# A LayerNorm over channels in a two-layer encoder: from transposes to sums by products with a constant matrix, with part of a weight's preparation moved to GpSimd

## The chip, the cores and the metric

One core of one Trainium2 chip runs the whole program. It has five engines with a queue each, and each queue is worked off in order: TensorE (PE in the profile; PEld is its loading of the stationary operand), VectorE (DVE), ScalarE (ACT), GpSimd (POOL) and SyncE (SP), which here issues the DMAs. They wait for each other by semaphores. The metric is the device time of one execution in microseconds (us); lower is better.

## The reference

Two layers over 256 tokens with 1024 features, in float32. Each layer is a SwiGLU feed-forward block (half step), a gated pair of token mixers side by side, a second SwiGLU block and a gated input embedding. The part that matters here is the convolution branch of the mixers, which ends in a LayerNorm over its 512 channels:

```python
def layer_norm(x, g, b, eps=1e-5):
    mu = jnp.mean(xf, axis=-1, keepdims=True)
    var = jnp.mean(jnp.square(xf - mu), axis=-1, keepdims=True)
    y = (xf - mu) * lax.rsqrt(var + eps)
    return (y * g + b)
...
        y_attn = window_attention(q, k, v, sink[i], rel_bias) @ w_attn_out[i]
        c_val, c_gate = jnp.split(c, 2, axis=-1)
        c = c_val * jax.nn.sigmoid(c_gate)
        c = depthwise_conv(c, conv_w[i], conv_b[i])          # 31 taps
        c = jax.nn.silu(layer_norm(c, conv_ln_g[i], conv_ln_b[i]))
        y_conv = c @ w_conv_out[i]
        g_attn, g_conv = jnp.split(jax.nn.sigmoid(g), 2, axis=-1)
        h = h + (g_attn * y_attn + g_conv * y_conv) @ w_o[i]
```

## The kernel before

**Layout.** Activations stand with features on the 128 partitions and the 256 tokens along the free axis, so a block of 128 features is a 128x256 tile. The 512 channels of the convolution are four such blocks, y[:, 0..3, :].

**Precision.** Matmuls run on float32r operands, and each float32 operand is split in a high part (a rounding copy on ACT) and a low part (the rest, by a subtraction on DVE); a product is three matmuls: high by high, high by low, low by high. The helper split does this for activations (line 489 is the subtraction: y_l, sum_l, ym_l). For weights the class Weights does it. A weight arrives by DMA in a buffer raw (five of them), ACT writes w_hi (line 136), DVE w_lo (line 137). A piece marked shared has its w_lo made by POOL instead, in four quarters (line 125). `ws.get()` hands out a piece and prepares pieces up to LOOK = 6 ahead, less `ws.rest`; `ws.behind` names an instruction behind which these preparations are put in their engines' queues.

**What sets the order.** The queues are filled by a scheduler that works from priorities and estimated times; where the code calls `keep_in_program_order` or `issue_after`, it is bound. Matmuls of one product (`group`) are followed by an evacuation that is put off until the first part of the next product.

**The mixers (function mix), in the order of TensorE.** Inner products for the convolution (ps_c), keys, values and queries, then the 16 gate blocks in pairs (ps_g; DVE multiplies them into g at line 910, ACT takes the sigmoid later in `squash`), between which the attention is worked off (ps_s, ps_pt, ps_o; o_h and o_l are the split of its result). Meanwhile DVE runs the 31 convolution taps for four blocks (line 669), 124 operations, the last tap of each block writing y. After the last gates come:

- attn_out(0, 2, 4, 6): the attention's output product in four groups of 24 matmuls (ps_ao), each followed by DVE's step g <- ps_ao * g (line 987).
- conv_out(0, 2, 4, 6): the convolution's output product in four groups of 24 (ps_co), reading y_h and y_l, each followed by two DVE steps (g <- ps_co * g, line 1061; the sum with the attention's share, line 1062) and the split into ym_h (ACT) and ym_l (DVE).
- mix_out: the product with w_o (ps_wo, 192 matmuls), reading ym; its first two blocks run over the first six of eight feature blocks each before the last two.

The LayerNorm lies between the attn_out groups. `ln_by_token`, after group 0, transposes y on TensorE so that tokens stand on the partitions (ps_yt, 8 transposes of 128x128), takes mean and variance with two statistics operations on DVE (BN_STATS, BN_AGGR), a square root on ACT over 128x2 values, a reciprocal over 128x2, and writes the normalised yn. `ln_by_channel`, half way through group 4, transposes back (ps_yc, 8 transposes), and ACT applies gain, bias and SiLU on the way out of PSUM (y, line 1028). y is split into y_h and y_l. ACT loads its function table twice for this, for Sqrt and for SiLU.

The kernel has the same scheme for RMS norms elsewhere, which the change borrows: ones_r is a 128x128 matrix of 1/1024, and two matmuls (sum_h and sum_l, ps_stat, line 455) put the sum over partitions of a 128x256 tile on every partition; a square root over 128x256 (sd, line 402) and a reciprocal over 128x256 (r_x, line 404) follow.

Of the kernel before, what the change touches and what calls it, by code (L numbers as in the profile page):

```python
# [48 lines left out]
G0, G1, G2, G3 = 56, 16, 8, 8  # L49
# [135 lines left out]
def encoder_kernel(ctx: ExitStack, tc: tile.TileContext, a: dict, out: bass.AP):  # L185
# [70 lines left out]
    def mix_specs(l):  # L256
# [28 lines left out]
        for j in range(2):  # L285
            u = ws.unit(KC, 512, w[j])
            for c in range(2):
                ws.spec(KC, 256, [(u, 0, c * 256, 0, 256)])
# [193 lines left out]
    def bcast(r, n):  # L482
        return r.unsqueeze(1).broadcast_to([P, n, T])
# [159 lines left out]
    def mix(l, u, st, xn, stat):  # L643
        cw, kg, bias, sink = (late[n] for n in ("cw", "kg", "bias", "sink"))
        with tc.tile_pool(name="mix_pool", bufs=1) as mp:
# [8 lines left out]
            last_tap = [None]  # L654

            def tap(i, t):
# [11 lines left out]
                else:  # L668
                    last_tap[0] = nc.vector.scalar_tensor_tensor(  # L669
# [139 lines left out]

            o = mp.tile([P, GROUP, P], F32, name="o")  # L810
# [58 lines left out]
            def gather(qb):  # L869
# [121 lines left out]
            yn = mp.tile([P, 2, CD], F32, name="yn", tag="sqq")  # L991

            def ln_by_token():
                mv = tmp.tile([P, 2, 2], F32, name="mv")
                ps = []
                for t in range(2):
                    ps.append(mm_tile("ps_yt"))
                    for i in range(KC):
                        turned = nc.tensor.transpose(ps[t][:, i * P : (i + 1) * P], y[:, i, t * P : (t + 1) * P], ident)
                        tc.keep_in_program_order(turned)  # L1000
                    six = tmp.tile([P, 6], F32, name="six")
                    nc.vector.bn_stats(out=six, in_=ps[t])
                    nc.vector.bn_aggr(out=mv[:, t, :], in_=six)
                rs = tmp.tile([P, 2], F32, name="rs")
                nc.scalar.activation(out=rs, in_=mv[:, :, 1], func=AF.Sqrt, bias=eps5)
                nc.vector.reciprocal(out=rs, in_=rs)
                table(AF.Silu)
                for t in range(2):
                    normed = nc.vector.tensor_scalar(
                        out=yn[:, t, :], in0=ps[t], scalar1=mv[:, t, 0:1], scalar2=rs[:, t : t + 1],  # L1010
                        op0=ALU.subtract, op1=ALU.mult,
                    )
                return (normed.ins,)
# [3 lines left out]
            def ln_by_channel():  # L1017
# [244 lines left out]
```

## Time and profile before

| | |
|---|---|
| device time, median of 3 runs | 1070.61 us (1070.31 to 1070.61) |
| the profiled execution | 1070.46 us, of which the span from the first to the last instruction is 1068.7 us |
| granted TensorE clock | 0.999 |
| busy share of the span | PE 99%, PEld 98%, DVE 76%, ACT 59%, POOL 12% |
| read from HBM | 200.46 MB, 189 GB/s over the span |

In the rows below, times are from the span's start. A timeline row gives start, length, engine, line and operation, what it writes and reads with shapes, how many instructions are merged, and in brackets the idle time before it with what ended that. A group's row gives the count, total busy time and mean duration in ns. Two instructions that follow each other directly on DVE or ACT overlap by 0.08 to 0.1 us in their records, so that the next starts before the last one's end is recorded. Chain rows stand at the ends of matmuls, timeline rows at their starts.

### The profile page before, as it was taken

How to read it: one execution, taken by the hardware profiler on the slowest of the kernel's cores; microseconds unless marked ns; L12 is line 12 of the kernel's file. 1: busy time of each engine (PE TensorE's matmuls, PEld its weight loads, DVE VectorE, ACT ScalarE, POOL GpSimd, SP SyncE). 2: the span in 40 equal slices, each digit the busy share in tenths (PEclk: the TensorE clock that was granted, in tenths of full speed). 3: DMA queues.
4: the chain of work that ended last, by engine and by line, in shares of the span. 5: the costliest groups of instructions: out<-in, count | busy, mean ns of one | idle time of the engine just before them, and what ended most of it. 6: DMA issues, size and time to landing. Idle time of an engine off the chain costs nothing.

```text
span 1068.7 us, 22087 instructions
## 1 busy us (share of the span) xinstructions
PE 1062.5 (99%) x9174; PEld 1048.2 (98%) x9174; DVE 813.2 (76%) x1234; ACT 627.3 (59%) x1043; POOL 130.4 (12%) x205
## 2 busy tenths in 40 slices
PE   9999999999999999999999999999999999999998
PEld 9999999999999999999999999999999999999998
DVE  7966666899899767666887766669998987666665
ACT  7655444777867554444774554548778675554453
POOL 0000011146301000011100000110571100000110
PEclk9999999999999999999999999999999999999999
DMA  9775555544256455555546454565433655454531
GB/s 368 269 266 178 183 205 214 190 167 158 98 205 238 182 202 184 182 201 219 188 169 223 171 198 142 214 237 197 159 130 112 227 214 216 180 192 144 218 119 40
DMA packets 30916, 202.93 MB, mean 190 GB/s; under 512 B 3552, under 2 KB 4832, under 8 KB 10464
## 3 DMA queue, kind: packets, MB, share of 16 engines
q1 hardware_dynamic: 30816, 201.52, 51.5%
q8 instruction: 72, 1.18, 0.4%
q14 instruction: 28, 0.23, 0.1%
HBM read 200.46 MB, written 1.05 MB: 189 GB/s over the span
## 4 chain that ended last, share of the span: by engine, by line
PE 92%; DVE 7%; ACT 1%; issue 0%; POOL 0%; DVEq 0%; ACTq 0%; POOLq 0%
PE ps_gu L330 43%; PE ps_fo L330 22%; PE ps_wo L330 4%; PE ps_pe L330 4%; PE ps_c L330 4%; DVE ps_y L669 4%; PE ps_g L330 2%; PE ps_ao L974 2%; PE ps_co L974 2%; PE ps_gu L343 2%; DVE s L835 1%; PE ps_pp L330 1%; DVE w_lo L137 1%; PE ps_q L779 1%; PE ps_q L778 1%; PE ps_q L777 1%
## 5 line engine op out<-in xcount | busy, mean ns | idle before, releaser
L136 ACT CAST w_hi<-raw 128x1024 fp32r<-128x1024 f32 (+2 forms) x364 | 372.7, 1031 | 354.5 <-PE ps_gu L330 198.4
L137 DVE TENSOR_TENSOR w_lo<-raw,w_hi 128x1024 fp32r<-128x1024 f32 (+2 forms) x364 | 433.9, 1199 | 187.3 <-ACT w_hi L136 187.2
L330 PE MATMUL ps_fo<-h_hi,w_lo 128*128 128x256 f32 x704 | 193.3, 275 | 0.0
L330 PE MATMUL ps_fo<-h_lo,w_hi 128*128 128x256 f32 x704 | 193.2, 275 | 0.0
L330 PE MATMUL ps_fo<-h_hi,w_hi 128*128 128x256 f32 x704 | 193.2, 275 | 0.0
L437 POOL TENSOR_TENSOR sq_acc<-sq_acc,sq 128x256 f32<-128x256 f32 x49 | 48.1, 981 | 803.3 <-ACT sq L436 803.3
L330 PEld LDWEIGHTS ps_fo<-h_lo,w_hi 128*128 128x128 f32 x704 | 131.9, 188 | 0.0
L330 PEld LDWEIGHTS ps_fo<-h_hi,w_hi 128*128 128x128 f32 x704 | 131.9, 188 | 0.0
L330 PEld LDWEIGHTS ps_fo<-h_hi,w_lo 128*128 128x128 f32 x704 | 131.9, 188 | 0.0
L330 PE MATMUL ps_gu<-xf0l,w_hi 128*128 128x256 f32 x352 | 96.9, 275 | 0.0
L330 PE MATMUL ps_gu<-xf1h,w_lo 128*128 128x256 f32 x352 | 96.9, 275 | 0.0
L330 PE MATMUL ps_gu<-xf0h,w_lo 128*128 128x256 f32 x352 | 96.9, 275 | 0.0
L330 PE MATMUL ps_gu<-xf1l,w_hi 128*128 128x256 f32 x352 | 96.9, 275 | 0.0
L330 PE MATMUL ps_gu<-xn0h,w_lo 128*128 128x256 f32 x352 | 96.8, 276 | 0.0
L330 PE MATMUL ps_gu<-xf0h,w_hi 128*128 128x256 f32 x352 | 96.8, 275 | 0.0
L330 PE MATMUL ps_gu<-xn0l,w_hi 128*128 128x256 f32 x352 | 96.8, 275 | 0.0
L330 PE MATMUL ps_gu<-xf1h,w_hi 128*128 128x256 f32 x352 | 96.8, 275 | 0.0
L330 PE MATMUL ps_gu<-xn0h,w_hi 128*128 128x256 f32 x352 | 96.7, 276 | 0.0
L669 DVE SCALAR_TENSOR_TENSOR ps_y<-cpad,cw,ps_y 128x256 f32<-128x256 f32 x232 | 95.5, 479 | 0.0
L330 PE MATMUL ps_gu<-x0h,w_hi 128*128 128x256 f32 x304 | 83.7, 275 | 0.0
L330 PE MATMUL ps_gu<-x0h,w_lo 128*128 128x256 f32 x304 | 83.7, 275 | 0.0
L330 PE MATMUL ps_gu<-x0l,w_hi 128*128 128x256 f32 x304 | 83.7, 275 | 0.0
(239 smaller groups left out, 2785.0 us busy)
## 6 DMA issues: line engine op xcount, KB each, us to landing
raw<-in_w_ffn_in_dram SPq DMA_DIRECT2D x86, 1024.0 KB, 4.9
raw<-in_w_ffn_out_dram SPq DMA_DIRECT2D x32, 896.0 KB, 4.6
raw<-in_w_in_dram SPq DMA_DIRECT2D x26, 1024.0 KB, 4.8
raw<-in_w_ffn_out_dram SPq DMA_DIRECT2D x16, 1024.0 KB, 5.3
raw<-in_w_o_dram SPq DMA_DIRECT2D x8, 1024.0 KB, 4.7
raw<-in_w_pe_gate_dram SPq DMA_DIRECT2D x8, 1024.0 KB, 4.9
raw<-in_w_q_dram SPq DMA_DIRECT2D x4, 1024.0 KB, 5.5
raw<-in_w_attn_out_dram SPq DMA_DIRECT2D x4, 1024.0 KB, 4.8
```

The lines of the kernel that those rows point to most:

```text
L136: lambda hs=hs, src=src: nc.scalar.copy(out=hs, in_=src),
L137: lambda hs=hs, ls=ls, src=src: nc.vector.tensor_tensor(out=ls, in0=src, in1=hs.bitcast(F32), op=ALU.subtract),
L330: mm = nc.tensor.matmul(ps, wa[:, k0 + k, cols], xa[:, kx, :], start=a, stop=b)
L343: mm = nc.tensor.matmul(ps, wa[:, k, :], xa[:, k, :], start=first and n == 0, stop=last and n == len(steps) - 1)
L437: nc.gpsimd.tensor_tensor(out=self.acc, in0=self.acc, in1=sq, op=ALU.add)
L669: last_tap[0] = nc.vector.scalar_tensor_tensor(out=ps if t < TAPS - 1 else y[:, i, :], in0=src, scalar=w, in1=ps, op0=ALU.mult, op1=ALU.add)
L777: nc.tensor.matmul(o_, u[0][:, kx, ts], wh[:, k, :], start=kx == 0, stop=False)
L778: nc.tensor.matmul(o_, u[0][:, kx, ts], wl[:, k, :], start=False, stop=False)
L779: nc.tensor.matmul(o_, u[1][:, kx, ts], wh[:, k, :], start=False, stop=kx == KD - 1)
L835: nc.vector.tensor_tensor_reduce(out=s[:, c, :], in0=ps[:, c, :], in1=bias[:, v * GROUP + c, off : off + T], scale=1.0, scalar=sink[:, hd ...
L974: mm = nc.tensor.matmul(ps[:, c, :], wa[:, k, c * P : (c + 1) * P], xa[:, k, :], start=(i, k) == (0, 0), stop=(i, k) == (2, KC - 1),)
```

## The change

The LayerNorm stays with channels on the partitions. Four blocks of y are added into one 128x256 tile (`over_blocks`: two, then one; DVE), the tile is split (`halve`: sum_h on ACT, sum_l on DVE) and two matmuls with ones_r give the sum over all channels on every partition (`spread`: ps_ln). `centre` subtracts the mean from y (yn, DVE, two operations on 128x512), squares on ACT, adds and halves again. `normalise` spreads the squares' sum, takes the root over 128x256 (sd, ACT), the reciprocal over 128x256 (r_ln, DVE), multiplies yn by it (DVE, two operations), applies gain, bias and SiLU from SBUF (ACT), and splits. The first sum is spread before attn_out(0), the second between attn_out(2) and attn_out(4). Table loads stay two a layer.

Besides, the first 256 columns' piece of the convolution's output weight (the first of four pieces of w_conv_out) gets its w_lo from POOL, and the points behind which weight pieces are prepared move: behind the first addition instead of the last tap, behind the centred sum's split, behind the new y's split. A gap in SBUF grows by the room of three small tiles that are gone.

```diff
-G0, G1, G2, G3 = 56, 16, 8, 8
+G0, G1, G2, G3 = 56, 64, 8, 8
...
         for j in range(2):
             u = ws.unit(KC, 512, w[j])
             for c in range(2):
-                ws.spec(KC, 256, [(u, 0, c * 256, 0, 256)])
+                ws.spec(KC, 256, [(u, 0, c * 256, 0, 256)], shared=j + c == 0)
...
+            def over_blocks(two, a, b):
+                nc.vector.tensor_tensor(out=two, in0=a, in1=b, op=ALU.add)
+                one = tmp.tile([P, T], F32, name="one", tag="sg")
+                made = nc.vector.tensor_tensor(out=one, in0=two[:, 0, :], in1=two[:, 1, :], op=ALU.add)
+                return one, made.ins
+
+            def halve(one):
+                parts = [tmp.tile([P, T], F32R, name="sum_" + part, tag="sq") for part in "hl"]
+                made = split(parts, one)
+                tc.keep_in_program_order(made[0])
+                return parts, tuple(ins.ins for ins in made)
+
+            def spread(parts):
+                ps = mm_tile("ps_ln")[:, :T]
+                for i, part in enumerate(parts):
+                    tc.keep_in_program_order(nc.tensor.matmul(ps, ones_r, part, start=i == 0, stop=i == 1))
+                return ps
...
                 made = nc.scalar.copy(out=oh[:, :, P:], in_=ov)
                 tc.keep_in_program_order(made)
+                sc["y"], _ = halve(sc.pop("y"))
                 for k in (0, 4, 8):
                     squash(k)
...
                 if i == 2 * KD - 2:
-                    ws.behind = (last_tap[0].ins,)
+                    two = tmp.tile([P, 2, T], F32, name="two", tag="gu")
+                    sc["y"], added = over_blocks(two, y[:, 0:2, :], y[:, 2:4, :])
+                    ws.behind = (added,)
                     last_gates(i)
...
-            def ln_by_token():
...
-            def ln_by_channel():
...
+            yn = mp.tile([P, KC, T], F32, name="yn", tag="sqq")
+
+            def centre():
+                ps, squares = spread(sc.pop("y")), []
+                flush()
+                for i in range(0, KC, 2):
+                    some = yn[:, i : i + 2, :]
+                    nc.vector.scalar_tensor_tensor(
+                        out=some, in0=bcast(ps, 2), scalar=-D / CD, in1=y[:, i : i + 2, :], op0=ALU.mult, op1=ALU.add
+                    )
+                    squares.append(tmp.tile([P, 2, T], F32, name="sq2", tag="gu"))
+                    tc.keep_in_program_order(nc.scalar.activation(out=squares[-1], in_=some, func=AF.Square))
+                squash(12)
+                sc["y"], made = halve(over_blocks(squares[0], *squares)[0])
+                table(AF.Sqrt)
+                return made
...
+            def normalise():
+                sd = tmp.tile([P, T], F32, name="sd", bufs=1)
+                root = nc.scalar.activation(
+                    out=sd, in_=spread(sc.pop("y")), func=AF.Sqrt, scale=D / CD, bias=eps5
+                )
+                tc.keep_in_program_order(root)
                 table(AF.Silu)
+                r = tmp.tile([P, T], F32, name="r_ln", tag="sg")
+                nc.vector.reciprocal(out=r, in_=sd)
                 for i in range(0, KC, 2):
+                    some = yn[:, i : i + 2, :]
+                    nc.vector.tensor_tensor(out=some, in0=some, in1=bcast(r, 2), op=ALU.mult)
+                    for k in range(i, i + 2):
                         act = nc.scalar.activation(
+                            out=y[:, k, :], in_=yn[:, k, :], func=AF.Silu,
+                            scale=pcol("conv_ln_g", l, k), bias=pcol("conv_ln_b", l, k),
                         )
...
-            ws.rest = 2
+            ws.rest, ws.behind = 2, centre()
             attn_out(0)
-            ws.rest, ws.behind = 2, (squash(12),) + ln_by_token()
+            ws.rest = 3
             attn_out(2)
-            ws.rest, made = 3, []
-            attn_out(4, lambda: made.extend(ln_by_channel()))
-            ws.rest, ws.behind = 2, tuple(made)
+            ws.behind = normalise()
+            attn_out(4)
             attn_out(6)
-            ws.rest = 3
```

How the queues stand around it in layer 1 (layer 2 reads alike). TensorE's queue from the last gate product on, before:

```order
L330 MATMUL ps_g<-xm0l,w_hi 128x256
L330 MATMUL ps_g<-xm0h,w_lo 128x256
L974 MATMUL ps_ao<-o_h,w_hi 128x256 x8
L974 MATMUL ps_ao<-o_h,w_lo 128x256 x8
L974 MATMUL ps_ao<-o_l,w_hi 128x256 x8
L999 MATMUL ps_yt<-ident,y 128x128 x8
```

And in the changed kernel:

```order
L330 MATMUL ps_g<-xm0l,w_hi 128x256
L330 MATMUL ps_g<-xm0h,w_lo 128x256
L826 MATMUL ps_ln<-sum_h,ones_r 128x256
L826 MATMUL ps_ln<-sum_l,ones_r 128x256
L996 MATMUL ps_ao<-o_h,w_hi 128x256 x8
L996 MATMUL ps_ao<-o_h,w_lo 128x256 x8
L996 MATMUL ps_ao<-o_l,w_hi 128x256 x8
```

The LayerNorm's first part now stands ahead of the attention output and not behind its first group; the other pair of ps_ln stands behind the second group.

VectorE's queue from the last two taps on, before:

```order
L669 SCALAR_TENSOR_TENSOR y<-cpad,cw,ps_y 128x256
L137 TENSOR_TENSOR w_lo<-raw,w_hi 128x1024
L669 SCALAR_TENSOR_TENSOR y<-cpad,cw,ps_y 128x256
L894 TENSOR_TENSOR o_l<-o,o_h 128x4x128
L894 TENSOR_TENSOR o_l<-ps_o,o_h 128x4x128
L910 TENSOR_TENSOR g<-ps_g,r_x 128x512
L987 TENSOR_TENSOR g<-ps_ao,g 128x512
L1002 BN_STATS six<-ps_yt 128x6 x2
L1003 BN_AGGR mv<-six 128x2 x2
L1006 RECIPROCAL rs<-rs 128x2
L1009 TENSOR_SCALAR yn<-ps_yt,mv,rs 128x512 x2
L137 TENSOR_TENSOR w_lo<-raw,w_hi 128x1024
```

In the changed kernel, first to the second sum:

```order
L668 SCALAR_TENSOR_TENSOR y<-cpad,cw,ps_y 128x256 x2
L811 TENSOR_TENSOR two<-y 128x512
L914 TENSOR_TENSOR o_l<-o,o_h 128x4x128
L813 TENSOR_TENSOR one<-two 128x256
L914 TENSOR_TENSOR o_l<-ps_o,o_h 128x4x128
L489 TENSOR_TENSOR sum_l<-one,sum_h 128x256
L930 TENSOR_TENSOR g<-ps_g,r_x 128x512
L1020 SCALAR_TENSOR_TENSOR yn<-ps_ln,y 128x512 x2
L1009 TENSOR_TENSOR g<-ps_ao,g 128x512
L811 TENSOR_TENSOR sq_3746<-sq_3746,sq_3749 128x512
L813 TENSOR_TENSOR one<-sq_3746 128x256
L489 TENSOR_TENSOR sum_l<-one,sum_h 128x256
```

and from there to the convolution output:

```order
L1009 TENSOR_TENSOR g<-ps_ao,g 128x512
L1040 RECIPROCAL r_ln<-sd 128x256
L1009 TENSOR_TENSOR g<-ps_ao,g 128x512
L1043 TENSOR_TENSOR yn<-yn,r_ln 128x512 x2
L1009 TENSOR_TENSOR g<-ps_ao,g 128x512
L489 TENSOR_TENSOR y_l<-y,y_h 128x512 x2
L137 TENSOR_TENSOR w_lo<-raw,w_hi 128x1024 x2
```

The preparation of the first convolution piece has left the queue, that of the second has moved behind y_l, and the step on the third ps_ao group stands between the reciprocal and the products that use it.

VectorE's queue at the end of the convolution output, with numbers: ps_co_3920, 3955 and 3988 are the second to fourth groups, ym_l0 and ym_l1 the low parts that ps_wo reads (two rows each, one for two feature blocks). Before:

```order
L1061 TENSOR_TENSOR g_3002<-ps_co_3920,g_3002 128x512
L489 TENSOR_TENSOR ym_l0_3891<-g_3002,ym_h0_3890 128x512
L1062 TENSOR_TENSOR g_3002<-g_3002 128x512
L1061 TENSOR_TENSOR g_3002<-ps_co_3955,g_3002 128x512
L1062 TENSOR_TENSOR g_3002<-g_3002 128x512
L489 TENSOR_TENSOR ym_l0_3891<-g_3002,ym_h0_3890 128x512
L1061 TENSOR_TENSOR g_3002<-ps_co_3988,g_3002 128x512
L489 TENSOR_TENSOR ym_l1_3893<-g_3002,ym_h1_3892 128x512
L1062 TENSOR_TENSOR g_3002<-g_3002 128x512
L489 TENSOR_TENSOR ym_l1_3893<-g_3002,ym_h1_3892 128x512
```

In the changed kernel, where the groups are 3925, 3960 and 3993:

```order
L1076 TENSOR_TENSOR g_3002<-ps_co_3925,g_3002 128x512
L1076 TENSOR_TENSOR g_3002<-ps_co_3960,g_3002 128x512
L489 TENSOR_TENSOR ym_l0_3892<-g_3002,ym_h0_3891 128x512
L1077 TENSOR_TENSOR g_3002<-g_3002 128x512 x2
L1076 TENSOR_TENSOR g_3002<-ps_co_3993,g_3002 128x512
L489 TENSOR_TENSOR ym_l0_3892<-g_3002,ym_h0_3891 128x512
L1077 TENSOR_TENSOR g_3002<-g_3002 128x512
L489 TENSOR_TENSOR ym_l1_3894<-g_3002,ym_h1_3893 128x512 x2
```

Before, the step on the last group had one ym_l directly behind it, the third; now it has the second, an addition, and then the third and the fourth.

More of the change, by code (lines that the diff above doesn't have):

```diff
@@ L653, in mix @@
             ws.lag = WEIGHTS_LAG
-            last_tap = [None]
             def tap(i, t):
@@ L668, in tap @@
                 else:
-                    last_tap[0] = nc.vector.scalar_tensor_tensor(
+                    nc.vector.scalar_tensor_tensor(
                         out=ps if t < TAPS - 1 else y[:, i, :], in0=src, scalar=w, in1=ps, op0=ALU.mult, op1=ALU.add
@@ L989, in attn_out @@
                 group([products], evac)
-            yn = mp.tile([P, 2, CD], F32, name="yn", tag="sqq")
-            def ln_by_token():
[L994 to L1006, printed above, removed]
-                table(AF.Silu)
[L1008 to L1013, printed above, removed]
@@ L1015, in mix @@
-            ys = tuple(rows(mp, KC, "y_" + part) for part in "hl")
-            def ln_by_channel():
-                banks = [mm_tile("ps_yc").rearrange("p (f t) -> p f t", f=2) for _ in range(2)]
-                for t in range(2):
-                    for k in range(KC):
-                        turned = nc.tensor.transpose(
-                            banks[k // 2][:, k % 2, t * P : (t + 1) * P], yn[:, t, k * P : (k + 1) * P], ident
-                        )
-                        tc.keep_in_program_order(turned)
+            yn = mp.tile([P, KC, T], F32, name="yn", tag="sqq")
@@ new lines, in centre @@
+            def centre():
[3 more added lines that the diff above has]
+                    some = yn[:, i : i + 2, :]
+                    nc.vector.scalar_tensor_tensor(
+                        out=some, in0=bcast(ps, 2), scalar=-D / CD, in1=y[:, i : i + 2, :], op0=ALU.mult, op1=ALU.add
[6 more added lines that the diff above has]
+                return made
@@ new lines, in mix @@
+            ys = tuple(rows(mp, KC, "y_" + part) for part in "hl")
+            def normalise():
[4 more added lines that the diff above has]
+                tc.keep_in_program_order(root)
+                table(AF.Silu)
+                r = tmp.tile([P, T], F32, name="r_ln", tag="sg")
+                nc.vector.reciprocal(out=r, in_=sd)
@@ L1025, in ln_by_channel @@
                 for i in range(0, KC, 2):
-                    ps = banks[i // 2]
-                    for f in range(2):
+                    some = yn[:, i : i + 2, :]
+                    nc.vector.tensor_tensor(out=some, in0=some, in1=bcast(r, 2), op=ALU.mult)
+                    for k in range(i, i + 2):
                         act = nc.scalar.activation(
-                            out=y[:, i + f, :], in_=ps[:, f, :], func=AF.Silu,
-                            scale=pcol("conv_ln_g", l, i + f), bias=pcol("conv_ln_b", l, i + f),
+                            out=y[:, k, :], in_=yn[:, k, :], func=AF.Silu,
+                            scale=pcol("conv_ln_g", l, k), bias=pcol("conv_ln_b", l, k),
```

## Prediction

> **What bounds the kernel now.** I read the page first (busy times, chain by engine), then the waits of TensorE, then the chain in order of time through the stretch that is changed, then the timelines of VectorE (DVE), ScalarE (ACT) and GpSimd (POOL) there.
>
> ```profile
> PE 1062.5 (99%) x9174; PEld 1048.2 (98%) x9174; DVE 813.2 (76%) x1234; ACT 627.3 (59%) x1043; POOL 130.4 (12%) x205
> ...
> PE 92%; DVE 7%; ACT 1%; issue 0%; POOL 0%; DVEq 0%; ACTq 0%; POOLq 0%
> ...
> PE ps_warm L218 <- POOL ones_d L211: 1.2, 1, 1.2
> PE ps_g L330 <- DVE o L884: 0.4, 2, 0.2
> ```
>
> TensorE is busy 99% of the span and is made to wait, as far as the records tell, three times for 1.6 us. So a matmul taken out shortens the kernel by its spacing, but any time for which TensorE comes to wait is added whole: there is no slack behind it. The profiled execution took 1070.46 us (span 1068.7 and 1.76 around it), 0.15 below the median of 1070.61; the sum starts from 1070.46. A change within 0.2% (2.1 us) can hardly be told from none.
>
> ```profile
> 282.96 2.73 PE ps_ao L974 x24
> 285.69 0.87 PE ps_yt L999 x8
> 286.56 4.10 PE ps_ao L974 x36
> 290.66 0.87 PE ps_yc L1021 x8
> ...
> 295.63 10.88 PE ps_co L974 x96
> 306.51 21.97 PE ps_wo L330 x192
> ...
> 336.64 0.24 PE ps_stat L455 x2
> ...
> 814.13 0.87 PE ps_yt L999 x8
> ...
> 819.11 0.87 PE ps_yc L1021 x8
> ```
>
> This chain (start, length, what) is TensorE without a break from the attention output (ps_ao) through the convolution output (ps_co) and the mixing output (ps_wo) to the next layer step. Layer 2 repeats it 528.4 us later, so everything below counts twice. A plain 128x128x256 matmul takes 10.88/96 = 0.113 us.
>
> **TensorE's own work.** Out go 16 transposes a layer: 0.87 + 0.87 = 1.74 us. In come four matmuls with the constant, like the pair ps_stat: 2 x 0.24 = 0.48. Net -1.26 a layer, -2.5 in all. This is the whole gain on offer; VectorE's convolution piece going to GpSimd frees no time on the chain by itself.
>
> **When the new sums are ready.** In the new order TensorE wants the first pair right behind the last ps_g, where ps_ao started before (282.80 on the timelines, whose starts lie 0.16 ahead of the chain's), and the second pair between the second and third ps_ao group.
>
> ```profile
> 279.29 0.47 DVE L669 SCALAR_TENSOR_TENSOR y<-cpad,cw,ps_y 128x256 f32<-128x256 f32 x1
> 279.68 1.21 DVE L137 TENSOR_TENSOR w_lo<-raw,w_hi 128x1024 fp32r<-128x1024 f32 x1
> 280.81 0.47 DVE L669 SCALAR_TENSOR_TENSOR y<-cpad,cw,ps_y 128x256 f32<-128x256 f32 x1
> 281.20 0.68 DVE L894 TENSOR_TENSOR o_l<-o,o_h 128x512 fp32r<-128x512 f32 x1
> ...
> L489 DVE TENSOR_TENSOR sum_l<-sq_acc,sum_h 128x256 fp32r<-128x256 f32 x8 | 3.4, 421 | 0.8 <-ACT sum_h L488 0.8
> L488 ACT CAST sum_h<-sq_acc 128x256 fp32r<-128x256 f32 x8 | 3.2, 406 | 6.4 <-POOL sq_acc L437 5.1 <-DVE sq_acc L553 1.2
> ...
> 272.62 5.65 POOL L125 TENSOR_TENSOR w_lo<-raw,w_hi 128x256 fp32r<-128x256 f32 x8 [1.62 <-ACT w_hi L122]
> 230.08 9.55 POOL L125 TENSOR_TENSOR w_lo<-raw,w_hi 128x256 fp32r<-128x256 f32 x12 [4.43 <-ACT w_hi L122]
> 230.35 0.75 DVE L684 TENSOR_TENSOR cpad<-sg,gu 128x256 f32<-128x256 f32 x1 [0.65 <-ACT sg L683]
> L684 DVE TENSOR_TENSOR cpad<-sg,gu x8: 410/418/755, 201.9 to 758.8; 128x256 f32<-128x256 f32 x8
> ```
>
> First pair. The w_lo that stood between the last two taps is gone (-1.13), so the second tap starts at 279.68 and ends at 280.15. Behind it stand, each 512-wide step 0.60 and each 256-wide 0.34 after the one before (durations 0.68 and 0.42): two at 280.18, o_l at 280.78, one at 281.38 (to 281.80), o_l at 281.72; ACT's sum_h 281.83 to 282.24; sum_l 282.33 to 282.75. TensorE wants sum_l at 282.80 + 0.11 = 282.91. That would just do, by 0.16. But the moved convolution piece gives POOL four more quarter operations of 5.65/8 = 0.71 behind those that end at 278.27, to about 281.1, beside two, o_l and one, which read both inputs from SBUF. No row shows these three beside POOL. The nearest is cpad: 0.42 alone, 0.75 beside POOL's w_lo. Below lies 0 (nothing collides), above 0.93 (two waits out the third quarter, 0.22, and o_l the whole fourth, 0.71). I take 0.5, a collision of cpad's size (0.34) and half of another; less the 0.16 it makes TensorE wait 0.3 (ends 0 and 0.8).
>
> [...]
>
> Second pair. TensorE comes to it at 282.80 + 0.24 + 0.4 + 5.44 = 288.88 (48 ps_ao at 0.113; 0.4 is the wait with its restart, below). The data need on ACT, behind sum_h at 282.74, three sigmoids, two squares, a sigmoid and the cast:
>
> ```profile
> 281.24 3.91 ACT L946 ACTIVATE g<-g 128x1024 f32<-128x1024 f32 x4
> 288.25 1.28 ACT L417 ACT_TABLE_LOAD   x1
> 291.35 1.02 ACT L1028 ACTIVATE y<-ps_yc,x 128x256 f32<-128x256 f32 x2 [1.82 <-PE ps_yc L1021]
> 292.40 0.62 ACT L488 CAST y_h<-y 128x512 fp32r<-128x512 f32 x1
> ...
> 293.98 0.62 ACT L488 CAST y_h<-y 128x512 fp32r<-128x512 f32 x1
> ...
> L548 ACT ACTIVATE sq<-x 128x512 f32<-128x512 f32 x2 | 1.1, 620 | 0.0
> L402 ACT ACTIVATE sd<-ps_stat,eps 128x256 f32<-128x256 f32 x8 | 3.8, 475 | 1.0 <-PE ps_stat L455 0.9
> L404 DVE RECIPROCAL r_x<-sd 128x256 f32<-128x256 f32 x8 | 14.0, 1752 | 2.5 <-ACT sd L402 2.5
> ```
>
> Sigmoids to about 285.5, squares to 286.6, then DVE's two adds (0.68, 0.42) behind its ps_ao step to 288.1, sum_h to 288.5, sum_l to 289.0: against 288.99 no wait worth counting.
>
> **The wait at the convolution output.** Behind the second pair TensorE has two ps_ao groups (5.44) and reaches ps_co at 288.88 + 0.24 + 5.44 = 294.56; its first matmul wants the first half of y_h, its third (294.8) the second. The way there: sum_h 288.5, table load 1.28 to 289.7, sd 0.48 to 290.2, the reciprocal, now of 128x256 and not of 128x2, 1.75 to 291.95. Next in DVE's queue stands the step on the third ps_ao (0.60; TensorE ends it at 291.84 and DVE can take it 0.2 later, so 0.1 is lost), and only behind it the two products with r_ln: the first ends at 291.95 + 0.1 + 0.60 + 0.68 = 293.3. Then ACT as in the rows above: from the first y to the end of the first y_h 1.67, to the end of the second 3.25 (294.60 - 291.35): 295.0 and 296.6. TensorE waits 0.4 and then until 296.6 instead of 294.8 + 0.4: 1.4 more, 1.8 in all. The old order had 1.0 to spare here (294.60 against 295.63). y is now read from SBUF and not from PSUM, which may save some hundredths on each of four; I take 1.7 (ends 1.3, if that and the queue are kind, and 2.0).
>
> **The wait at the mixing output.** The squeezed-out w_lo make DVE late through ps_co, and the new order puts DVE's four last steps differently: the second ym_l now stands behind the step on the last ps_co, and a g add before the third ym_l.
>
> ```profile
> 306.55 0.69 DVE L1061 TENSOR_TENSOR g<-ps_co,g 128x512 f32<-128x512 f32 x1 [0.37 <-PE ps_co L974]
> 307.15 0.68 DVE L489 TENSOR_TENSOR ym_l<-g,ym_h 128x512 fp32r<-128x512 f32 x1
> ...
> 306.35 0.28 PE L330 MATMUL ps_wo<-ym_h,w_hi 128*128 128x256 f32 x1
> ...
> 307.70 0.28 PE L330 MATMUL ps_wo<-ym_h,w_hi 128*128 128x256 f32 x1
> 307.89 0.38 PE L330 MATMUL ps_wo<-ym_l,w_hi 128*128 128x256 f32 x1
> 308.11 0.28 PE L330 MATMUL ps_wo<-ym_h,w_lo 128*128 128x256 f32 x1
> ```
>
> Before, ps_wo began at W = 306.35, DVE's step on the last ps_co at W + 0.20, and the ym_l that the 14th matmul reads came at W + 1.48: 307.89 - 307.70 is 0.08 more than the spacing, a wait that the list above does not even show, and the next gap is 0.22, 0.11 lost in restarting. Now W + 0.20 is followed by ym_l (0.80 to 1.48), the add (1.41) and the ym_l for the 14th matmul (2.01 to 2.70). The 8th matmul, due at W + 0.79, waits for the first of these until 1.51 (0.7); the 14th, then due at 2.3, until 2.73 (0.45). Together 1.15, less the 0.08 of before: +1.07 (ends 0.8 and 1.3).
>
> Restarts: 0.11 at each of five pauses (one at ps_ln, two at ps_co, two at ps_wo), one of them old: +0.4.
>
> **What I cost at nothing.**
>
> ```profile
> L136 ACT CAST w_hi<-raw 128x1024 fp32r<-128x1024 f32 (+2 forms) x364 | 372.7, 1031 | 354.5 <-PE ps_gu L330 198.4
> 289.92 1.21 DVE L137 TENSOR_TENSOR w_lo<-raw,w_hi 128x1024 fp32r<-128x1024 f32 x1
> raw<-in_w_o_dram SPq DMA_DIRECT2D x8, 1024.0 KB, 4.7
> ```
>
> VectorE's queue grows by the reciprocal's 1.75 and several steps of 0.4 to 0.7, less the old statistics and one w_lo; what covers it is that weight pieces are prepared ahead. The cover is thin at one place: the w_lo of the second ps_co piece comes at 296.5 + 1.03 + 1.21 = 298.7, and TensorE wants it at 296.6 + 22 x 0.113 = 299.1; any lateness would be paid whole. Later pieces come every 1.13 us, and TensorE uses one in 2.7. That w_lo was done at 291.1 before, so the load on SP's queue that reuses its buffer goes out 7.6 us later and lands at about 303.4 (4.7 each); it brings the last two of eight w_o pieces, wanted 16 us after ps_wo begins, so the loads behind it on that queue are no nearer to their use either. POOL's piece is ready 13 us before its use. The longer gap memset ahead of ones_d, for which TensorE waits at the start, costs some hundredths once; where tiles come to lie in SBUF I price at zero, as no row shows a price for it.
>
> **Sum.** A layer: -1.26 + 0.3 + 1.7 + 1.07 + 0.4 = +2.2; two layers +4.4; 1070.46 + 4.4 = 1074.9 us.
>
> **Rivals.**
> The gain comes through. All waits are covered and only -2.5 stays: 1068.0. For it speaks that the old chain had 1.0 us to spare at ps_co; against it that y_h would have to come 1.8 earlier, which is just the reciprocal's length, and the ym_l order would have to be harmless as well. It decides from the point where both waits together fall below 1.26 a layer. 7%.
> One wait alone. The convolution output waits but the mixing output doesn't (DVE could have run its adds sooner), or the other way round: -1.26 + 0.3 + 1.7 + 0.2 = +0.9, or -1.26 + 0.3 + 1.07 + 0.2 = +0.3 a layer: 1071.1 to 1072.3, no difference to speak of. Against it: the two have separate causes, both in fixed queues. 13%.
> GpSimd holds VectorE. If each of two, o_l and one waits out a quarter, the first pair waits 0.8, and a late w_lo at the second ps_co adds 0.3: +3.0 a layer, 1076.5. The rows of cpad speak for the kind, not for the number of collisions. [...] 15%.
> The likeliest, both waits and a small collision: 65%, with bounds from the low ends (-1.26 + 0 + 1.3 + 0.8 + 0.3 = +1.1, 1072.7) to the high ends without the third rival (+2.9, 1076.3).
>
> **The numbers.** 1074.9. The range of 8 in 10 takes in the likeliest case (65%), the third rival (to 1077.2) and the upper edge of the second (1071.9): 1071.9 to 1077.2. Faster by over 0.2%: 0.07; within 0.2%: 0.14; slower: 0.79.
>
> **What would show it.** In the changed kernel's list of TensorE waits: ps_co for ACT's y_h, about 1.5 to 1.8 us twice; ps_wo for DVE's ym_l, about 0.7 and 0.4 twice; ps_ln for DVE's sum_l, up to 0.8. From ps_wo to the next ps_stat nothing changes. If ps_co starts at 294.6 and runs 10.9 us without a break, the step on the reciprocal is wrong; if ps_wo still takes 22.0 us, the step on the ym_l order is.

## The result, and the profile after

The changed kernel takes 1078.16 us (median of four executions, 1076.63 to 1080.1) against 1070.56 before (1070.31 to 1070.61): a ratio of 1.0073 [1.0061, 1.0085], slower by 7.6 us. The forecast was 1074.9 (1071.9 to 1077.2): the sign is right, the time lies above the range. The profiled execution is the fastest of the four: 1076.63 us, a span of 1074.8 against 1068.7.

The page's busy times and the chain by engine:

```profile
PE 1063.2 (99%) x9150; PEld 1046.6 (97%) x9150; DVE 819.7 (76%) x1240; ACT 630.9 (59%) x1051; POOL 136.3 (13%) x213
...
PE 87%; DVE 10%; ACT 2%; DMA 0%; issue 0%; SPq 0%; DVEq 0%; ACTq 0%
```

TensorE still looks busy 99% of the time (a matmul's record is mostly 0.28 long and its spacing 0.113, so short pauses hide in that number). But the chain is TensorE for 87% instead of 92% of the span: it now runs through other engines. The list of TensorE's waits names them (total us, times, longest):

```profile
PE ps_co L996 <- ACT y_h L488: 3.2, 4, 1.1
PE ps_wo L330 <- DVE ym_l L489: 1.6, 4, 0.6
PE ps_warm L218 <- POOL ones_d L211: 1.2, 1, 1.2
PE ps_gu L343 <- ACT w_hi L136: 0.4, 1, 0.4
```

The two new waits are those that the prediction names, in both layers; the last row is a wait of 0.4 at the kernel's start. (A fifth row, 0.4 at ps_g, stands as before.) Through the changed stretch the chain, which was TensorE without a break, now reads (start, length, what):

```profile
280.94 1.22 DVE o_l L914
282.16 0.34 DVE one L813
...
283.09 0.34 DVE sum_l L489
283.44 0.04 issue
...
289.49 0.39 PE ps_ln L826
...
292.66 0.69 DVE g L1009
293.36 0.61 DVE yn L1043
...
293.99 1.10 ACT y L1045 x2
...
296.76 0.63 ACT y_h L488
...
297.43 10.97 PE ps_co L996 x94
...
310.97 20.61 PE ps_wo L330 x179
331.58 8.16 PE ps_gu L330 x72
339.74 0.24 PE ps_stat L455 x2
...
871.16 0.24 PE ps_stat L455 x2
```

The stretch begins with the last gate product. Before, TensorE's timeline has there:

```profile
282.69 0.28 PE L330 MATMUL ps_g<-xm0h,w_lo 128*128 128x256 f32 x1
282.80 0.95 PE L974 MATMUL ps_ao<-o_h,w_hi 128*128 128x256 f32 x7
```

From the last ps_g (282.81, below) to ps_stat it is 56.93 us; before, from the last ps_g (282.69) to ps_stat (336.64), 53.95. So a layer costs 2.98 more. The second layer agrees: ps_stat comes 531.42 after that of the first layer instead of 528.45, 2.97 more. With the 0.12 by which the last ps_g comes later this is the whole difference of the spans, 6.1. TensorE's timeline of the changed kernel shows the pauses themselves (start, length, and in brackets the idle time by the modelled ends; the plain spacing is 0.113):

```profile
282.81 0.28 PE L330 MATMUL ps_g<-xm0h,w_lo 128*128 128x256 f32 x1
282.99 0.38 PE L826 MATMUL ps_ln<-sum_h,ones_r 128*128 128x256 f32 x1
283.48 0.39 PE L826 MATMUL ps_ln<-sum_l,ones_r 128*128 128x256 f32 x1
283.70 0.28 PE L996 MATMUL ps_ao<-o_h,w_hi 128*128 128x256 f32 x1
...
289.18 0.28 PE L826 MATMUL ps_ln<-sum_h,ones_r 128*128 128x256 f32 x1
289.49 0.39 PE L826 MATMUL ps_ln<-sum_l,ones_r 128*128 128x256 f32 x1
...
295.07 0.28 PE L996 MATMUL ps_ao<-o_l,w_hi 128*128 128x256 f32 x1
295.79 0.50 PE L996 MATMUL ps_co<-y_h,w_hi 128*128 128x256 f32 x2 [0.44 <-ACT y_h L488]
297.43 0.62 PE L996 MATMUL ps_co<-y_h,w_hi 128*128 128x256 f32 x3 [1.14 <-ACT y_h L488]
...
308.90 0.28 PE L330 MATMUL ps_wo<-ym_h,w_hi 128*128 128x256 f32 x1
309.77 0.38 PE L330 MATMUL ps_wo<-ym_l,w_hi 128*128 128x256 f32 x1 [0.59 <-DVE ym_l L489]
...
310.46 0.28 PE L330 MATMUL ps_wo<-ym_h,w_hi 128*128 128x256 f32 x1
310.97 0.39 PE L330 MATMUL ps_wo<-ym_l,w_hi 128*128 128x256 f32 x1 [0.23 <-DVE ym_l L489]
```

The start of a delayed matmul less the start of the one ahead of it and 0.113 is the pause: 0.38 and 0.20 at ps_ln, 0.61 and 1.30 at ps_co (for the latter 297.43 - 295.79 less two spacings and the 0.11 of the restart before), 0.75 and 0.40 at ps_wo. (The first ps_ln comes 0.07 late as well.) Behind each of the six the next matmul starts 0.22 later instead of 0.113.

This explains 1076.6, not 1078.2. What sets the other executions apart had no place in the prediction, and the first experiments are about it.

### The profile page after: what moved, and what is told of

It is laid out like the page before. It is cut to its first block, busy times and chain, and to the rows that moved or that the text cites. A ratio compares the mean times of both kernels' runs of the same rounds, so it can differ in the third digit from the quotient of the medians.

```text
span 1074.8 us, 22065 instructions
## 1 busy us (share of the span) xinstructions
PE 1063.2 (99%) x9150; PEld 1046.6 (97%) x9150; DVE 819.7 (76%) x1240; ACT 630.9 (59%) x1051; POOL 136.3 (13%) x213
## 4 chain that ended last, share of the span: by engine, by line
PE 87%; DVE 10%; ACT 2%; DMA 0%; issue 0%; SPq 0%; DVEq 0%; ACTq 0%
PE ps_gu L330 43%; PE ps_fo L330 22%; DVE ps_y L668 6%; PE ps_pe L330 4%; PE ps_c L330 4%; PE ps_wo L330 4%; PE ps_co L996 2%; PE ps_ao L996 2%; PE ps_gu L343 1%; DVE s L854 1%; PE ps_pp L330 1%; DVE g L930 1%; DVE w_lo L137 1%; PE ps_q L778 1%; PE ps_q L776 1%; PE ps_q L777 1%
```

## Experiments

### Where the slower executions come from

Nothing is edited in the first of these four.

> The changed kernel once more, for its spread: four executions so far gave 1076.6, 1078.0, 1078.4 and 1080.1 us, where the kernel before stays within 0.3. Theory (clock): the new pauses of TensorE in the convolution output (0.6 and 1.3 us, 1.6 apart) make the throttle grant a lower clock for a short stretch in some executions, at about 1.7 us each, at most once a layer. Then the times fall into steps: 1076.6, about 1078.3 and about 1080.1, with granted clocks of 0.999, 0.998 and 0.996, and a profile of a slower execution shows a stretch of some 3.4 us at half clock right behind those pauses. Rival (other cause): the spread comes from transfers or from when the engines meet; then the times lie anywhere between 1076 and 1081, and the clock is 0.999 in all.

Measured: 1076.30, 1077.83, 1078.06, 1078.17 and 1080.16 us; ratio 1.0071 [1.0058, 1.0083]. With the four from before, nine executions stand on three steps: two at 1076.3 to 1076.6, five at 1077.8 to 1078.4, two at 1080.1 to 1080.2, with mean granted clocks of 0.999 to 1.0, 0.998 and 0.996. The profiled execution (1078.17) is one of the middle step. The table by stretches (busy time and count of PE, PEld, DVE, ACT, POOL; then the granted clock, the DMA share and GB/s):

```profile
294.41:297.82 3.41, 1.83 (x14) 1.43 (x13) 1.84 (x4) 3.35 (x7) 0.00 (x0) 1.00 0.00 0
297.82:301.23 3.41, 3.41 (x19) 3.41 (x18) 2.65 (x3) 3.41 (x5) 0.00 (x0) 0.50 0.23 38
...
826.88:830.29 3.41, 1.95 (x15) 1.55 (x14) 1.95 (x4) 3.26 (x7) 0.00 (x0) 1.00 0.00 0
830.29:833.70 3.41, 3.29 (x28) 3.29 (x29) 3.05 (x4) 3.41 (x5) 0.00 (x0) 1.00 0.13 19
```

Right behind the two ps_co pauses of layer 1 the clock column reads 0.50 for 3.41 us (a drop, below), and only 19 matmuls touch that stretch, where 32 do in a busy stretch at full clock (a row further down). From the last ps_g to ps_stat, start to start, layer 1 takes 58.29 us and layer 2 56.76: the half clock costs 1.5 here, near the 1.7 that half of 3.41 would be, and that is the step. In layer 2 of the same execution the same pauses lie a little otherwise to the 3.41 us stretches (busy 1.95, not 1.83), and nothing follows. The next kernel keeps the waits and takes the idleness out of them:

```diff
+    def idle(n, ps, w, x):
+        for _ in range(n):
+            tc.keep_in_program_order(nc.tensor.matmul(ps, w, x, start=True, stop=True))
...
+                        if (name, f) == ("ps_co", 0):
+                            idle({0: 5, 2: 11}.get(n, 0), ps[:, 1, :], wh[:, 0, :P], o_parts[0][:, 0, :])
```

> The changed kernel, in which TensorE does needless products with finished operands into a bank that is overwritten afterwards while it would wait: 5 ahead of the first and 11 ahead of the third ps_co product, 6 and 3 ahead of the 8th and the 14th ps_wo product, each 0.113 us. The waits stay as long, only TensorE isn't idle in them. Theory (clock): no lower clock any more, so all executions within 0.5 us of each other at 1075.8 to 1077.0 with a clock of 0.999; the restarts of 0.11 may shrink as well, up to 0.4 a layer. Rival (other cause): the spread of 1076.6 to 1080.1 stays as it is.

Measured: 1076.33 to 1077.58 us (median 1076.56; ratio 1.0058 [1.0045, 1.007]), the clock 0.999 or 1.0 in all five. (Needless products stand ahead of the two ps_wo products in the same way.) The upper steps are gone, the median falls by 1.5 and the fastest stays. The restarts did not shrink: from the last ps_g to ps_stat, start to start, this kernel takes 56.81 and the changed one 56.77. One execution lies above the expected 1077.0. It was profiled, and has its delay at the kernel's start: a wait of 1.4 us at the first ps_gu, which is between nothing and 0.8 in the profiles of the other kernels. So the steps come from TensorE resting, not from transfers. Does it take this change to do so? The next two put a pause into the kernel before:

```diff
-                    for f in range(2):
+                    for f in (0, 0, 1, 1) if i == 0 else (0, 0, 1):        # pause
+                    for f in (0, 0, 1, 1) if i == 0 else (0, 0, 0, 1, 1, 1):   # long
                         act = nc.scalar.activation(out=y[:, i + f, :], in_=ps[:, f, :], func=AF.Silu, ...
```

> The kernel before, with three of the four Silu instructions of the convolution's norm given twice a layer (1.02 us each on ScalarE), so that the second y_h comes at 297.7 instead of 294.6 and TensorE, which wants it at 295.85, waits about 1.85 us once a layer with 0.11 to restart. Nothing of the change is in it. By the pauses alone: 1070.5 + 2 x 1.96 = 1074.4 us. Theory (clock): that is the fastest execution, and others lie about 1.7 or 3.4 above it with clocks of 0.998 and 0.997, though one pause may do it less often than two. Rival (other cause): all within 0.5 us of 1074.4 with a clock of 0.999.

Measured: 1072.38 us (1071.91 to 1072.69, eleven executions), ratio 1.0017 [1.0008, 1.0026], no step. The pause came out at 0.6 by the waits list and not 1.85: the 1.02 of the timeline row that the expectation went by is the time of the two instructions merged in it, so each repeat adds 0.55. As a test of the clock this says only that one pause of 0.6 a layer does nothing to it.

> The kernel before, with the Silu instructions of the convolution's norm repeated more often (4 and 6 instructions for 2 and 2, 0.55 us each), so that TensorE has one pause of about 2.25 us a layer at the third ps_co product; nothing of the change is in it. With the pause of 0.6 (the run with seven instead of ten) eleven executions took 1071.9 to 1072.7 us without a step. By the pauses alone: 1072.3 + 2 x 1.65 = 1075.6 us. Theory (clock): the throttle looks at stretches of 3.41 us (the records last 3.413) and gives half clock for the next when TensorE rested for more than about half of one; a pause of 2.25 lies in one stretch far enough in more than half of all executions: steps of 1.7, at 1075.6, 1077.3 and 1079.0, more executions above the first than on it. Rival (the change itself, its two pauses close together or its instructions, does it): all within 0.8 of 1075.6, clock 0.999.

Measured: 1077.48, 1077.80, 1079.17, 1079.27 and 1079.32 us, ratio 1.0074 [1.0061, 1.0087], clocks 0.998, 0.998 and three times 0.997. The waits list gives the pauses as 4.8 us in two, the longest 2.4. From start to start the pause is 2.54 a layer, with 0.11 to restart; by the pauses alone that is 1070.65 + 2 x 2.65 = 1076.0, not 1075.6. No execution is left there; they stand one and two steps above it. The profiled one (1077.80):

```profile
293.87:297.28 3.41, 2.33 (x21) 2.13 (x19) 1.50 (x3) 3.28 (x7) 0.00 (x0) 1.00 0.46 195
297.28:300.70 3.42, 2.12 (x18) 2.12 (x19) 1.88 (x3) 3.35 (x6) 0.00 (x0) 1.00 0.02 5
826.34:829.76 3.42, 1.04 (x10) 0.84 (x9) 0.84 (x3) 3.29 (x7) 0.00 (x0) 1.00 0.10 41
829.76:833.17 3.41, 3.41 (x16) 3.41 (x17) 3.16 (x4) 3.41 (x4) 0.00 (x0) 0.50 0.00 0
```

In layer 1 the same pause falls across the boundary of two stretches, leaving 2.33 and 2.12 busy, and no half clock follows; in layer 2 it falls in one (1.04), and it does. That settles it: the step needs nothing of the change but the pause.

The two records of half clock in the run without GpSimd's subtractions (below) begin at 297.38 and 829.86, 156 times 3.413 us apart, and the records of full clock in the kernel before and the changed one last 311 and 313 times as long (1061.54 and 1068.37): the records stand on a grid of 3.413 us. It starts at another point in each execution (in layer 1 a stretch begins at 294.41 above and at 295.37 below). In the middle of the kernels profiled, a stretch of the grid with TensorE busy for 1.84 us or less was followed by one at half clock (five stretches, in four kernels), and one with 1.85 or more was not: where the last expectation has "about half", the least rest that brought it was 1.57 us (46%). The line can't be drawn finer than this, since the ends of matmuls are modelled, and where a kernel begins or ends it does not hold everywhere (last section). Among these, the changed kernel's own profile, without a drop, has the nearest miss:

```profile
295.37:298.78 3.41, 1.85 (x13) 1.65 (x14) 2.40 (x4) 3.38 (x6) 0.00 (x0) 1.00 0.00 0
298.78:302.20 3.42, 3.42 (x32) 3.42 (x32) 3.42 (x4) 3.42 (x5) 0.00 (x0) 1.00 0.43 127
```

So in layer 1 of the run again two pauses, 0.61 and 1.30 by the changed kernel's profile, were enough in a stretch that was busy for 1.83.

### The terms of the sum

Does GpSimd hold VectorE at o_l? GpSimd's subtractions for the moved piece go, and with them their reads:

```diff
+                if self.next_prep in self.empty:      # the moved piece
+                    nc.gpsimd.memset(lv.bitcast(F32), 0.0)
+                    ...
+                    continue
                 for a in range(0, k, k // QUARTERS):
```

> The changed kernel without GpSimd's four subtractions for the moved convolution piece; that low part is set to zero by one memset on GpSimd instead, so the piece's second part is left out of the product. Theory (collision): o_l beside GpSimd (1.22 us) goes back to 0.68, sum_l comes 0.5 earlier, TensorE's first pause at ps_ln (0.38 us beyond the spacing) all but goes: 0.4 a layer, fastest execution 1075.8 against 1076.6. Rival: the long o_l has nothing to do with GpSimd (it is on the path for other reasons): o_l stays at 1.2 and the time at 1076.6. The waits at ps_co (1.9 a layer) and ps_wo (1.2) stay by both.

Measured: 1076.95 us (1075.39 to 1079.04, on the same steps; the profiled one has a drop in each layer), ratio 1.0055 [1.0041, 1.0069]. VectorE's timeline has:

```profile
281.23 0.69 DVE L920 TENSOR_TENSOR o_l<-o,o_h 128x512 fp32r<-128x512 f32 x1
```

o_l takes 0.69 instead of 1.22 beside GpSimd; the first pair runs without a pause, the fastest execution is 0.9 faster than the changed kernel's (1076.30). The collision is real and costs 0.53, near the 0.5 that was taken. The timelines of the changed kernel show how it comes about:

```profile
280.30 0.71 DVE L811 TENSOR_TENSOR two<-y 128x512 f32<-128x512 f32 x1
280.39 1.22 POOL L125 TENSOR_TENSOR w_lo<-raw,w_hi 128x256 fp32r<-128x256 f32 x1
```

GpSimd's last quarter begins while two runs and is recorded at 1.22, where the quarter before it took 0.77. o_l begins at 280.94, while this quarter runs (to 281.61), and takes 1.22. By these records each of the two is held by the one that began ahead of it. The sum one begins after that and takes its 0.41.

Next, the order ahead of ps_wo. VectorE's step on the last ps_co is queued behind the third ym_l, and ScalarE's weight piece behind the third ym_h:

```diff
+                    with ExitStack() as queue:
+                        if f == KD - 2:
+                            queue.enter_context(tc.issue_after(lows[-1]))
+                        nc.vector.tensor_tensor(out=gs, in0=ps, in1=gs, op=ALU.mult)
...
+                    if f == KC:
+                        ws.behind += (highs[2],)
```

> The changed kernel with the queues ahead of ps_wo put otherwise: VectorE's step on the last ps_co stands behind the third ym_l instead of ahead of the second, and ScalarE casts the third ym_h ahead of a weight piece instead of behind it. Theory (order): the ym_l that the 8th ps_wo product reads comes 0.6 earlier and the one that the 14th reads as well, so the pauses of 0.75 and 0.4 shrink to 0.2 together: 1.2 a layer less, fastest execution 1076.3 - 2.3 = 1074.0 us; the ps_co pauses and with them the steps of 1.7 for the lower clock stay (1074.0 to 1077.5). Rival (backlog): VectorE is behind by the weight pieces that came later, whatever the order; the wait goes to another ym_l and the fastest stays above 1075.5.

Measured: 1074.41 us, and 1076.05 to 1077.13 in the other four, which have a drop; ratio 1.0049 [1.0035, 1.0063]. ps_wo is gone from the waits list, a gap of 0.13 beyond the spacing is left. The one execution without a drop gives 1.9 of the 2.3 back. The order was the cause, not the backlog.

The reciprocal:

```diff
-                table(AF.Sqrt)
+                tc.keep_in_program_order(nc.scalar.preload_act_table_set('natural_log_exp_and_others'))
...
-                root = nc.scalar.activation(out=sd, in_=spread(sc.pop("y")), func=AF.Sqrt, scale=D / CD, bias=eps5)
...
-                nc.vector.reciprocal(out=r, in_=sd)
+                root = nc.scalar.activation(out=sd, in_=spread(sc.pop("y")), func=AF.Ln, scale=D / CD, bias=eps5)
+                tc.keep_in_program_order(nc.scalar.activation(out=r, in_=sd, func=AF.Exp, scale=-0.5))
```

> The changed kernel with 1/sqrt made on ScalarE as exp(-0.5 ln(v)) (one table load for both, two instructions of about 0.48 us) instead of a square root there and a reciprocal of 1.75 us on VectorE. Theory (the reciprocal sets y_h): the products with r_ln start at about 291.5 instead of 293.3, the first y_h comes at about 293.7 and the second at 295.4 instead of 297.4, which is when TensorE wants it: the ps_co pauses (1.9 with 0.2 of restarts a layer) go to 0.2 or less, and with them the lower clock; ps_wo's 1.15 stay: all executions at 1072.2 to 1073.3 us, clock 0.999. Rival (moved wait): with the reciprocal gone VectorE's weight pieces or the Silu table load keep y_h or ym_l late; then ps_wo takes over more than half of it, 1074.5 or more.

Measured: 1073.17 to 1074.05 us in five executions and 1075.04 in the profiled sixth, which has its half clock at 8.2 us, at the kernel's start; ratio 1.0031 [1.0019, 1.0043]. Its waits:

```profile
PE ps_wo L330 <- DVE ym_l L489: 1.6, 4, 0.6
...
PE ps_co L996 <- ACT y_h L488: 0.8, 2, 0.4
```

By the list the wait at ps_co falls from 3.2 to 0.8, ps_wo keeps its own, and no drop follows in the middle of the kernel. The fastest execution is 3.1 us faster than the changed kernel's; most of the others lie above the expected 1072.2 to 1073.3. Not all of this is the reciprocal's own time: in this kernel VectorE's step on the third ps_ao (0.69) stands behind the products with r_ln, where the changed kernel has it ahead of them. What is left at ps_co is ScalarE's queue: its table load for SiLU (1.28), which the reciprocal (1.75) had covered, now ends at 293.93, 0.57 after the first product with r_ln (293.36).

One half of the change alone, in the kernel before: GpSimd's share.

```diff
-G0, G1, G2, G3 = 56, 16, 8, 8
+G0, G1, G2, G3 = 56, 64, 8, 8        # not in share16
...
-                ws.spec(KC, 256, [(u, 0, c * 256, 0, 256)])
+                ws.spec(KC, 256, [(u, 0, c * 256, 0, 256)], shared=j + c == 0)
```

> The kernel before with the second part of the first convolution output piece on GpSimd, which is one half of the change alone (with the longer gap that goes with it). Theory: it frees VectorE by 1.13 us where TensorE doesn't wait for it (the norm's transposes stand 3 us later), and the collision with o_l (0.54) is hidden as well: no change, 1070.3 to 1070.9 us. Rival (POOL part costs): GpSimd's four quarters hold VectorE or reach ps_co late: 1071.2 or more. The other half, the norm, then carries all of the loss.

Measured: 1087.75 us (1087.32 to 1088.13), ratio 1.0159 [1.0144, 1.0173]: a miss of both. No wait is new. A group of the page before, and then two groups of the share's page and two pieces of its chain:

```profile
L330 PE MATMUL ps_fo<-h_hi,w_lo 128*128 128x256 f32 x704 | 193.3, 275 | 0.0
...
L330 PE MATMUL ps_fo<-h_hi,w_lo 128*128 128x256 f32 x704 | 197.1, 281 | 0.0
L330 PE MATMUL ps_gu<-xf0h,w_lo 128*128 128x256 f32 x352 | 96.8, 275 | 0.0
...
310.61 22.83 PE ps_wo L330 x192
333.44 8.22 PE ps_gu L330 x72
```

ps_wo takes 22.83 for the 21.97 of before, ps_fo's matmuls 281 ns for 275; ps_gu's are as they were. The experiment had changed two things: with the gap, everything behind it moves up by 48 elements, 192 bytes. In the whole change six small tiles of the old norm (three, in two buffers each) go at the same place, nothing moves, and ps_fo's matmuls take 275.

> The run with GpSimd's share alone took 1087.4 to 1088.1 us, 17 more than before, with no new wait on TensorE: the products of ps_fo, ps_wo and ps_pe take 281 ns there instead of 275. That kernel had two edits: the share, and the gap of 64 elements for 16, which puts everything behind it 192 bytes further up in SBUF (in the whole change the gap stands in for six small tiles that go, and nothing moves). This is the share with the gap left at 16. Theory (place): the 17 us come from the 192 bytes, and the share costs nothing: 1070.3 to 1070.9 us, 275 ns. Rival (share): GpSimd's four quarters slow TensorE's reads: 1087 again.

Measured: 1070.59 us (1070.37 to 1070.99, eleven executions), ratio 0.9999 [0.999, 1.0008]. So the share costs nothing by itself, and the 17 us came with the 192 bytes. (The move without the share was not run.)

### Versions that put it together

Both mends in one kernel, the edits of the order and of the reciprocal as above:

> The changed kernel with both mends so far: the reciprocal as exp(-0.5 ln(v)) on ScalarE, and the queues ahead of ps_wo put otherwise. Alone they took the fastest execution from 1076.3 to 1073.2 and to 1074.4. Theory (separate waits): they add up, 1076.3 - 3.1 - 1.9 = 1071.3, and since no 3.41 us hold more than about 0.6 us of pause there is no lower clock in the middle: all executions at 1071.0 to 1072.2 us. Rival (one backlog): the second mend finds nothing left or the pause at ps_co grows: 1072.7 or more.

Measured: 1071.39 us (1071.18 to 1072.22, eleven executions), ratio 1.0008 [0.9999, 1.0017], no drop. They add up: the waits are separate, and with them mended nearly the whole loss is undone (0.7 us of 7.6 is left). For a gain the chain from the last tap to y_h has to be shorter:

```diff
-                for k in (0, 4, 8):
+                for k in (0, 4):
                     squash(k)
...
+                    with tc.issue_after(ins):          # one, and sum_l for the second
                         nc.vector.tensor_tensor(out=ol[:, :, s], in0=src, in1=oh[:, :, s].bitcast(F32), op=ALU.subtract)
...
+                squash(8)
                 squash(12)
```

> The kernel with both mends, and the chain ahead of ps_co shortened: VectorE adds the second time (one) ahead of o_l and splits the sum (sum_l) ahead of the second o_l, and ScalarE does the third sigmoid of the gates behind the two squares instead of ahead of them. Theory (the chain from the last tap to y_h sets the rest): sum_l comes about 0.6 earlier, the squares 1.0 earlier, the second y_h at about the time at which TensorE wants it; pauses of 0.3 or less a layer are left, so the 16 transposes less come through: 1070.6 - 2 x 1.26 + 0.2 to 0.8 = 1068.3 to 1068.9 us, clock 0.999. Rival (another wait): VectorE's weight pieces or o_l for ps_ao's third pass come late instead: 1070.5 or more.

Measured: 1069.74 us (1069.39 to 1070.39), ratio 0.9992 [0.9983, 1.0002]: between the two. Both pairs at ps_ln run without a pause, a pause at the third ps_co is left (the waits list has 0.8 in two). The collision moved on: one, now in o_l's place beside GpSimd's last quarter, takes 0.85 instead of 0.42.

```diff
+                squash(0)                                                  # ahead of the second o_h
                 made = nc.scalar.copy(out=oh[:, :, P:], in_=ov)
...
+                        if f == 0:
+                            queue.enter_context(tc.issue_after(sc["sum"]))   # the first ps_ao step, behind one
```

> The kernel of the run before (1069.7 us, one pause of 0.55 with its restart of 0.11 at the third ps_co product left in each layer, 0.24 at ps_wo) with three more steps moved: the first sigmoid of the gates ahead of the second o_h (ScalarE rests 1.08 there), the third back ahead of the squares (it rests 0.4 there), and VectorE's second addition of the squares (one) ahead of its step on the first ps_ao. Theory (ScalarE's queue sets y_h now): the sum's cast comes 0.6 earlier, and so the second y_h, 0.05 or less behind TensorE: 1069.7 - 2 x 0.6 = 1068.5 us (1068.2 to 1069.0), faster than before by 0.2%. Rival (the second pair of sums sets it, which TensorE itself reaches at its own pace): the square root starts no earlier, 0.3 a layer or less: 1069.1 or more.

Measured: 1069.06 us (1068.60 to 1069.90, eleven executions) against 1070.68: 0.9985 [0.9976, 0.9994], the clock 1.0 in all eleven. Its TensorE waits are the old ones:

```profile
PE ps_warm L218 <- POOL ones_d L211: 1.2, 1, 1.2
PE ps_g L330 <- DVE o L903: 0.4, 2, 0.2
PE ps_gu L343 <- ACT w_hi L136: 0.2, 1, 0.2
```

The time lies between theory (1068.5) and rival (1069.1 or more), at the rival's edge, and the cause that the profile shows is the rival's: the square root now waits 0.17 for the second pair, and the chain runs from there through the root, the exponential, the table load and SiLU to the second y_h. 0.2 at ps_co and 0.15 at ps_wo are left. So of the 2.5 us that the 16 transposes less are worth by count, 1.6 come through when the waits are mended.

## Why the prediction was wrong

By its own terms, a layer (forecast, and what the changed kernel's profile shows):

| term | forecast | measured |
|---|---|---|
| TensorE's own work | -1.26 | -1.26, by count |
| first pair at ps_ln | +0.3 | +0.38, and 0.07 ahead of it |
| second pair | 0 | +0.20 |
| ps_co waits for y_h | +1.7 | +1.91 |
| ps_wo waits for ym_l, less 0.08 | +1.07 | +1.07 |
| restarts at 0.11 | +0.4 | +0.55 (six pauses, not five) |
| sum | +2.2 | +2.92 (2.98 by the stretch) |

**The mechanisms were right.** Each wait came at the matmul, for the tile and from the engine that the prediction named; the ps_wo term is right to 0.01, and undoing the order took the wait away. ps_wo to ps_stat is unchanged, as it said. What was costed at nothing held: TensorE waited for no weight piece in the changed stretch, GpSimd's share alone measured nothing, and the tiles did not move, so the place in SBUF cost nothing here.

**Small terms, all missed on the same side.** The second pair had been placed with nothing to spare (sum_l at 289.0 against 288.99, "no wait worth counting"); with no slack anything late is paid, and it was 0.20 and a restart. ps_co had been credited with SiLU reading SBUF instead of PSUM ("some hundredths on each"): y took 1.10 for two, not less than 1.02, and no run shows that saving. Together 0.7 a layer, 1.4 in all: 1070.46 + 2 x 2.92 + 0.12 gives 1076.4 of the 1076.63 that the profiled execution took. That is inside the range, and so are both executions without a drop.

**The step that failed** is that a pause was priced at its length and a restart of 0.11. Two pauses of 1.91 together within 2.4 us also bring half clock for the next 3.41 us when they fall in one stretch of the grid, at 1.5 to 1.7 a time: by their times, in nine of eighteen layers of the nine executions. The median has one such drop, and that is what lifts it out of the range. The prediction's profile, in which the clock stayed at 1.00 from 5.13 to 1066.67 of 1068.7 us, could not show this: with TensorE busy 99% of the time, nothing in it could say what a pause does to the clock. The prediction has no term for the clock, and its range had no room for one.

**The rivals.** GpSimd holding VectorE is half right. Of the three instructions only o_l is held, by 0.53: it takes 0.69 without GpSimd's reads and 1.22 with them. GpSimd's last quarter takes 1.22 behind two. The upper end of 0.8 was not reached because two came ahead of that quarter and one after it (0.71 and 0.41, against 0.69 and 0.41 without GpSimd's reads). That this rival's 1076.5 is what the executions without a drop took is luck: of its two terms, 0.8 at the first pair and 0.3 for a late w_lo, the first measured 0.45 and the second nothing. One wait alone and the gain coming through are refuted.

## What to carry to other kernels

When TensorE is the bound and runs without a break, price each wait that a change brings at its length plus a restart (0.11 here). Then ask whether it and its neighbours can fall into one 3.41 us stretch of the clock's grid and leave TensorE busy for 1.84 us of it (54%) or less; in the middle of these kernels half clock followed all five such stretches, and cost another 1.5 to 1.7 each. A pause that falls across the boundary of two stretches escaped once (layer 1 of the run with one long pause); spreading or splitting pauses on purpose was not tried. Count a forecast that leaves no slack as a wait. And an experiment that undoes half of a change must leave the tiles where they were (192 bytes cost 17 us here).

## What the runs showed of the hardware that was not expected

- In the middle of the kernels, half clock for 3.413 us after a grid stretch in which TensorE was busy for 1.84 us or less, and none after 1.85 (by records whose ends are modelled). Two cases outside the middle stay open: in the kernel with the logarithm a half-clock record begins at 8.20 us, among the kernel's first matmuls, behind a stretch that was busy for 2.60; and in the kernel with the order mended the stretch with TensorE's last matmuls, from 1068.49, is busy for 1.84 and the clock stays full behind it.
- Moving tiles by 192 bytes in SBUF cost 17 us: the matmuls of ps_fo, ps_wo and ps_pe, whose moving operands lie behind the gap, took 281 to 283 ns instead of 275 to 277 (those of ps_ao, ps_co and ps_pp slowed by as much); those of ps_gu (the first few at the kernel's start aside) and of ps_g, whose moving operands lie ahead of it, did not change. Why is not settled.
- A matmul that had waited was followed by the next 0.22 us later instead of 0.113, at each of the six pauses in a layer, and also where needless products filled the pause.
